# Reordering waits and splits in a two-layer decoder trunk in split float32

## The chip, the cores and the metric

One Trainium2 chip, one core. The metric is the device time of one execution in microseconds (us); lower is better. Times of several executions are given as a median.

## The reference

Two layers run over a sequence of 512 tokens of width 1024. Each layer is one pre-normalised mixer, a residual add, and a gated per-layer embedding:

```python
u = rms_norm(h, norm_g)
z = u @ w_in                       # q,k,v,gate of 8 "fox" heads, forget column, q,k,v,gate of 8 dilated heads
log_f = log_sigmoid(fa + b_f)      # forget logarithm, 8 heads
oa = forgetting_attention(rms_norm(qa), rms_norm(ka), va, log_f) * silu(ga)   # bias: cumulated log_f, causal
ob = dilated_attention(rope(rms_norm(qb)), rope(rms_norm(kb)), vb) * silu(gb)
h = h + concat([oa, ob]) @ w_out
gate = sigmoid(rms_norm(h, ple_norm_g) @ w_ple_gate)
h = h + (p_i @ w_ple) * gate
```

Everything is float32. The kernel keeps that precision on TensorE by cutting each operand into a rounded high half and the low half that is left, and by three products (high by high, high by low, low by high) in place of one.

## The kernel before

**Tiling.** Activations lie transposed, 8 blocks of 128 channels by 512 tokens; the tiles `X` and `Y` each hold a high and a low half of all 8 blocks. The 16 heads are taken as 8 pairs: pairs 0 to 3 are dilated heads, pairs 4 to 7 forgetting heads. Tokens come in 4 tiles of 128.

**Weights.** The class `Weights` (lines 93 to 201) streams them in a fixed order. A piece is loaded by SP into one of 3 `raw` buffers, ScalarE copies it into a high half `whi` (line 159), VectorE subtracts to get the low half `wlo` (line 160). There are 5 slots of halves. `W.pump()` does one piece if a slot is free, and issues the next load; `W.get` does pieces until the one asked for is there. Each piece that is done frees a raw buffer, and so lets the next load go.

**The order of the work.** TensorE's instructions keep the order in which they are written (`InOrder`, line 80). The other engines' instructions are put in order by a planner, which simulates the program at compile time and takes what is ready, what is written earlier first; at run time each engine's queue is then fixed. `with behind("A", "V"):` (line 372) pins what is issued inside it on ScalarE ("A") and VectorE ("V") behind the instructions recorded in `last["A"]` and `last["V"]`. These records are made at a few places only: line 449 (copy of v), 456 and 464 (q and k after the norm and the rotation), 480 (gate), 620 and 621 (halves of the probabilities), 650 and 651 (output of a product with v), 810 (the low half of a weight piece), and 881 (the embedding gate).

**A layer.** First pair 0 is projected (`proj`) into four PSUM banks, two of the pool `psA` and two of `psM`; in layer 0 this goes block by block as the inputs arrive (lines 664 to 692), and for block `d == 0` all four token tiles take one of the three products before the next product begins. Then for p from 1 to 7 (line 753) pair p is projected in four tiles (`pj`, `ev`), the scores and the softmax of pair p - 1 are made (`att_s`), its probabilities are transposed (`att_tp`, `att_tp2`) and split (`att_pt`, `att_pt2`), and pair p - 2 is multiplied with v (`att_pv`) and written out as halves (`att_o`). `bias_causal` adds the causal mask to the bias rows of a forgetting pair in two VectorE instructions (line 529); `att_s` adds the mask rows to the scores and takes the minimum (line 596), ScalarE takes the exponential (598), VectorE a reciprocal (599), GpSimd scales (600).

**The forget logarithm.** `log_forget` (line 484) makes log_f of 128 by 32 elements with two table functions of ScalarE, Exp and Ln; `cumulate`, at p = 4, first splits it (lines 501 and 502) and then sums it along the tokens. `rope_tables(l + 1)` makes the rotation tables of the next layer in 8 VectorE instructions (lines 366 and 367). Both are written into the loop without a pin, at p = 2 and at p = 7.

**The last pair and the output product.** From line 815 on the output product (`part(d, k0, k1)`) runs on the blocks of pairs that are done, between the last steps of attention: `att_pv` of pair 6, `att_o(6)`, the scores of pair 7, `part(0, 6, 7)`, which needs both halves of pair 6's output, `part(2, 0, 5)`, and the transposes of pair 7's probabilities. After the eight output blocks comes the embedding gate, a loop over d: `pgate(d)` is the product with the gate weights into a bank of `psA`, `gated` reads it on VectorE (line 881), ScalarE takes Tanh (882), VectorE multiplies and adds (886, 888); in layer 0 the block is stored (`hs`), split for the next layer (391, 392) and squared. Each d ends with one pump whose instructions on VectorE are pinned behind line 881 of the same d:

```python
                with behind("V"):
                    W.pump()
```

The next layer's first projection starts right after the last `pgate`.

Of the kernel before, what the change touches and what calls it, by code (L numbers as in the profile page):

```python
# [9 lines left out]
F32 = mybir.dt.float32  # L10
F32R = mybir.dt.float32r
I32 = mybir.dt.int32
AF = mybir.ActivationFunctionType
ALU = mybir.AluOpType
# [189 lines left out]
def trunk(tc, ap):  # L204
# [3 lines left out]
    with ctx:  # L208
# [275 lines left out]
        def log_forget(l):  # L484
            t = [sp.tile([P, NT, 8], F32, tag=f"lf{i}", name=f"lf{i}", bufs=1) for i in range(4)]
            y, w, lw, e = t
            V.tensor_scalar(y, fx, -1.0, None, op0=ALU.mult)
            V.tensor_tensor(y, y, fx, op=ALU.max)
            A.activation(y, y, AF.Exp, scale=-1.0)
            V.tensor_scalar(w, y, 1.0, None, op0=ALU.add)  # L490
            A.activation(lw, w, AF.Ln)
            V.tensor_scalar(e, w, 1.0, None, op0=ALU.subtract)
            V.tensor_tensor(e, y, e, op=ALU.subtract)
            V.reciprocal(w, w)
            V.tensor_tensor(e, e, w, op=ALU.mult)
            V.tensor_tensor(lw, lw, e, op=ALU.add)
            V.scalar_tensor_tensor(fx, fx, 0.0, lw, op0=ALU.min, op1=ALU.subtract)

        def cumulate():
            ps = ptile(psM, "psM")  # L500
            A.activation(lf[:, :, 0:8], fx, AF.Copy)
            V.tensor_tensor(lf[:, :, 32:40], fx, lf[:, :, 0:8].bitcast(F32), op=ALU.subtract)
            for t in range(NT):
                n = (NT - t) * P
                T.matmul(ps[0:40, S - n:], lf[:, t], tri[:, :n], start=(t == 0),
                         stop=(t == NT - 1))
            c = tp.tile([8, S], F32, tag="ob", name="c")
            A.activation(c, ps[32:40], AF.Copy)
            V.tensor_tensor(c, ps[0:8], c, op=ALU.add)
            nc.sync.dma_start(cd, c)  # L510
# [15 lines left out]

        def bias_causal():
            for x in (MF[:, 7:20:4], MF[:, 3:13:3]):
                V.tensor_tensor(x, x, causal[:, None, :].to_broadcast([P, NT, P]), op=ALU.add)  # L529

# [119 lines left out]

        def att_o(a, dst):
            V.tensor_tensor(U[7], U[7], U[5 + a % 2], op=ALU.mult)  # L654
            A.activation(dst[0][:, a], U[7], AF.Copy)
            V.tensor_tensor(dst[1][:, a], U[7], dst[0][:, a].bitcast(F32), op=ALU.subtract)  # L656


        gh, oo = X, Y
# [5 lines left out]
        for d in range(NK):  # L665
            if d == 0:
                W.slice_conv()
                with tc.issue_after(W.first.ins):
                    split_gh(gh, U[d], gn[:, 0, d:d + 1], d)
            else:  # L670
                split_gh(gh, U[d], gn[:, 0, d:d + 1], d)
                W.slice_conv()
            if d == 2:
                W.slice_load()
                W.slice_load()
                small_loads()
            tail = square_acc(U[d], d)
            if d == NK - 1:
                while W.load():
                    pass  # L680
                W.pump(PZ)
                stats0 = finish_stats(psS, "psS")
                rope_base(tail)
                rope_tables(0)
            if d == 0:
                wh, wl = (x[:, :QW0] for x in W.cur)
                for i in range(3):
                    for t in range(NT):
                        T.matmul(first[t][:, :QW0], gh[i % 2][:, 0, t * P:(t + 1) * P],
                                 wl if i == 2 else wh, start=i == 0, stop=False)  # L690
            for t in range(NT if d > 0 else 0):
                proj(0, 0, t, gh, first[t], d, d + 1)
        for l in range(DEPTH):
            u = gh
# [57 lines left out]

            for p in range(1, NPAIR):
                a, b = p - 1, p - 2
                if p == 2:
                    log_forget(l)
                if p == 7 and l + 1 < DEPTH:
                    rope_tables(l + 1)
                if p == 1:
                    pj(p, 0)  # L760
                    pj(p, 1)
                    ev(p, 0)
                    att_qk(l, 0, att_z(zt(0)))
                    W.pump(2)
                else:
                    pj(p, 0, 0, 6)
                    att_pv(b, 0)
                    att_pt(1, tps)
                    pj(p, 0, 6, NK)
                    pj(p, 1, 0, 3)  # L770
                    att_pv(b, 1)
                    pj(p, 1, 3, NK)
                    ev(p, 0)
                    with behind("A", "V"):
                        W.pump()
                    att_o(b, oo)
                ev(p, 1)
                if p > 1:
                    with behind("A", "V"):
                        W.pump()  # L780
                if a >= NDIL:
                    with behind("V"):
                        bias_causal()
                pj(p, 2)
                ev(p, 2)
                att_s(a)
                if NDIL <= p < NPAIR and a >= NDIL:
                    bias_rows(p)
                pj(p, 3)
                ev(p, 3)  # L790
                if p == NDIL:
                    cumulate()
                    bias_rows(p)
                gps = ptile(psA, "psA")
                gate_mm(l, p, u, gps, 0, NK)
                with behind("A", "V"):
                    W.pump()
                tps = [pair(psS, "psS") for _ in range(2)]
                att_tp(tps)
                pqk = att_z(zt(p))  # L800
                tpb = ptile(psA, "psA")
                att_tp2(tpb)
                tanh, rest = gate_evac(p, gps)
                att_pt(0, tps)
                with behind("A"):
                    tanh()
                att_pt2(tpb)
                with behind("A", "V"):
                    W.pump()
                last["V"] = W.lo  # L810
                att_qk(l, p, pqk)
                with behind("V"):
                    rest()
# [3 lines left out]
            att_pv(b, 0)  # L817
            att_pt(1, tps)
            with behind("A", "V"):
                W.pump()  # L820
            part(0, 5, 6)
            part(1, 0, 3)
            att_pv(b, 1)
            with behind("A", "V"):
                W.pump()
            part(1, 3, 5)
            att_o(b, oo)
            with behind("V"):
# [39 lines left out]

            def pgate(d, k0, k1, c=slice(0, S)):
                if d not in gps or c.start > 0:  # L870
                    gps[d] = ptile(psA, "psA")
                wh, wl = W.get(("pg", l, d))
                for k in range(k0, k1):
                    mm3(gps[d][:, c], wh[:, k, :], wl[:, k, :], pg[0][:, k, c], pg[1][:, k, c],
# [29 lines left out]
            for d in range(NK):  # L904
# [25 lines left out]
                else:  # L930
# [5 lines left out]
                    for c, th in zip(halves, ths):  # L936
                        ple(d, c)
                        gated_b(d, c, th)
                        nc.sync.dma_start(ap["out"][d][:, c], U[d][:, c])
                with behind("V"):  # L940
                    W.pump()
            gh, oo = nxt, pg


# [54 lines left out]
```

## Time and profile before

| what | value |
|---|---|
| median of 3 runs | 700.66 us (699.09 to 1112.28) |
| the profiled execution, its own time | 699.79 us |
| its span, first to last instruction | 698.0 us |
| mean granted TensorE clock | 0.997 |
| HBM read, written | 70.78 MB, 4.23 MB |
| DMA, mean | 109 GB/s |

A line of the profile that groups instructions gives line, engine, operation, output and inputs by tile name, then busy time and the idle time of the engine ahead of them with what ended it. PE is TensorE's matmuls, PEld its weight loads, DVE VectorE, ACT ScalarE, POOL GpSimd, SPq the queue of SP. `L87` and `L90` are the two helpers through which all matmuls and all transposes go, so these are told apart by their tiles. PE's busy time is modelled, so PE counts as busy between closely spaced matmuls; the start times of its instructions show its real pace.

### The profile page before, as it was taken

What the parts mean: (1) busy time and instruction counts of PE and PEld (TensorE: products, weight loads), DVE (VectorE), ACT (ScalarE), POOL (GpSimd) and SP (SyncE); (2) the same over time, 40 slices, a digit from 0 to 9 for tenths busy, and PEclk for the clock granted to TensorE, in tenths of its full rate; (3) what the DMA queues carried; (4) which work ended last, traced back from release to release, by engine and by line L of the source; (5) the groups of instructions that cost most, each with busy time, mean ns of one, the idle gap of its engine ahead of it and who ended that gap; (6) DMA issues with size and microseconds to landing.
All of it is one profiled execution on the core that took longest, in us unless ns stands there. A gap on an engine that the chain in (4) does not pass through costs nothing.

```text
span 698.0 us, 12101 instructions
## 1 busy us (share of the span) xinstructions
PE 688.7 (99%) x4351; PEld 612.2 (88%) x4351; DVE 512.1 (73%) x1255; ACT 381.2 (55%) x806; POOL 181.0 (26%) x318
## 2 busy tenths in 40 slices
PE   9999999999999999999989999999999999999997
PEld 8998898999989878888789998999989998788887
DVE  7888788777887878638558678777878877784544
ACT  8676556565664766435325566466555756573311
POOL 7462634324131220000003625534041331200000
PEclk9999999999999999999999999999999999999999
DMA  7612232234342444414253032221543533453221
GB/s 254 225 33 69 56 93 66 83 113 156 96 137 98 130 134 154 136 45 146 98 167 121 1 91 65 87 69 54 155 127 111 138 107 120 130 159 105 91 76 46
DMA packets 32172, 75.79 MB, mean 109 GB/s; under 512 B 4832, under 2 KB 12256, under 8 KB 32112
## 3 DMA queue, kind: packets, MB, share of 16 engines
q1 hardware_dynamic: 31824, 75.01, 34.4%
q8 instruction: 34, 0.56, 0.3%
q14 instruction: 26, 0.21, 0.1%
q10 hardware_dynamic: 288, 0.01, 0.0%
HBM read 70.78 MB, written 4.23 MB: 107 GB/s over the span
## 4 chain that ended last, share of the span: by engine, by line
PE 91%; DVE 4%; ACT 2%; issue 1%; POOL 1%; DMA 1%; SPq 0%; DVEq 0%; ACTq 0%; POOLq 0%
PE psA L87 63%; PE psS L87 19%; PE psM L87 4%; PE psS L90 2%; PE psM L90 1%; PE psA L90 1%; DVE wlo L160 1%; ACT U L598 1%; POOL f L443 1%; DMA raw<-in_wq_dram 1%; DVE MF L529 0%; DVE U L596 0%; DVE U L654 0%; ACT whi L159 0%; DVE z L456 0%
## 5 line engine op out<-in xcount | busy, mean ns | idle before, releaser
L159 ACT ACTIVATE whi<-raw 128x1024 fp32r<-128x1024 f32 (+5 forms) x104 | 106.3, 1024 | 63.6 <-PE psA L87 41.9
L160 DVE TENSOR_TENSOR wlo<-raw,whi 128x1024 fp32r<-128x1024 f32 (+3 forms) x105 | 123.3, 1174 | 13.8 <-ACT whi L159 13.0
L87 PE MATMUL psA<-whi,X 128*128 128x384 f32 (+1 forms) x480 | 130.7, 342 | 0.9 <-DVE U L480 0.9
L87 PE MATMUL psA<-whi,Y 128*128 128x384 f32 (+1 forms) x480 | 129.9, 342 | 0.0
L443 POOL TENSOR_TENSOR f<-ms,mhalf 128x4 f32<-128x4 f32 x64 | 64.7, 1011 | 237.7 <-DVE ms L441 228.3
L87 PE MATMUL psA<-Y,whi 128*128 128x512 f32 (+1 forms) x320 | 97.0, 386 | 0.8 <-DVE Y L656 0.7
L87 PE MATMUL psA<-X,whi 128*128 128x512 f32 x304 | 96.3, 397 | 0.8 <-DVE X L656 0.6
L598 ACT ACTIVATE U<-U,mx 128x512 f32<-128x512 f32 (+3 forms) x128 | 70.5, 553 | 40.4 <-DVE mx L596 30.3
L87 PEld LDWEIGHTS psA<-whi,X 128*128 128x128 f32 x480 | 87.4, 188 | 2.2 <-DVE U L480 0.9
L87 PEld LDWEIGHTS psA<-whi,Y 128*128 128x128 f32 x480 | 87.5, 188 | 0.6
L87 PE MATMUL psA<-wlo,X 128*128 128x384 f32 (+1 forms) x240 | 80.9, 338 | 0.2 <-DVE wlo L160 0.2
L87 PE MATMUL psA<-wlo,Y 128*128 128x384 f32 (+1 forms) x240 | 81.0, 338 | 0.0
L600 POOL TENSOR_SCALAR U<-U,sm 128x512 f32<-128x512 f32 (+3 forms) x128 | 65.7, 531 | 51.0 <-DVE sm L599 50.7
L87 PEld LDWEIGHTS psA<-Y,whi 128*128 128x128 f32 x320 | 58.4, 188 | 13.7 <-DVE Y L656 1.0
L87 PEld LDWEIGHTS psA<-X,whi 128*128 128x128 f32 x304 | 56.5, 188 | 14.5 <-DVE X L656 1.0
L87 PE MATMUL psA<-Y,wlo 128*128 128x512 f32 (+1 forms) x160 | 61.1, 382 | 0.0
L87 PE MATMUL psA<-X,wlo 128*128 128x512 f32 x152 | 60.0, 395 | 0.0
L620 ACT ACTIVATE PT<-psS 128x512 fp32r<-128x512 f32 (+1 forms) x58 | 31.3, 590 | 50.9 <-PE psS L90 39.0
L456 DVE TENSOR_TENSOR z<-psA,f 128x256 f32<-128x256 f32 x60 | 25.4, 423 | 40.6 <-POOL f L443 40.6
L405 POOL TENSOR_TENSOR r<-m,mhalf 128x4 f32<-128x4 f32 x4 | 4.7, 1184 | 162.5 <-DVE m L404 162.5
L87 PEld LDWEIGHTS psA<-wlo,X 128*128 128x128 f32 x240 | 45.1, 188 | 0.5 <-DVE wlo L160 0.5
L87 PEld LDWEIGHTS psA<-wlo,Y 128*128 128x128 f32 x240 | 45.2, 188 | 0.0
(187 smaller groups left out, 1240.3 us busy)
## 6 DMA issues: line engine op xcount, KB each, us to landing
raw<-in_wq_dram SPq DMA_DIRECT2D x28, 576.0 KB, 3.9
raw<-in_wg_dram SPq DMA_DIRECT2D x16, 512.0 KB, 3.5
raw<-in_wo_dram SPq DMA_DIRECT2D x16, 512.0 KB, 3.3
raw<-in_wpg_dram SPq DMA_DIRECT2D x16, 512.0 KB, 3.4
raw<-in_wq_dram SPq DMA_DIRECT2D x14, 384.0 KB, 3.2
U<-in_xT_dram SPq DMA_DIRECT2D x16, 256.0 KB, 4.2
MF<-cd SPq DMA_DIRECT2D x16, 256.0 KB, 3.5
MF<-cd SPq DMA_DIRECT2D x16, 192.0 KB, 3.7
```

The lines of the kernel that those rows point to most:

```text
L87: return self.tc.keep_in_program_order(self.eng.matmul(*a, **k))
L90: return self.tc.keep_in_program_order(self.eng.transpose(*a, **k))
L159: self.nc.scalar.activation(hi, r, AF.Copy)
L160: self.lo = eng.tensor_tensor(lo, r, hi.bitcast(F32), op=ALU.subtract)
L405: G.tensor_tensor(r, m, mhalf.to_broadcast([P, NT]), op=ALU.pow)
L443: G.tensor_tensor(f, ms, mhalf.to_broadcast([P, 4]), op=ALU.pow)
L456: last["V"] = V.tensor_tensor(z, ps[:, :2 * P].rearrange("p (h d) -> p h d", h=4), f[:, :, None].to_broadcast([P, 4, HD]), op=ALU.mult)
L598: A.activation(seg, seg, AF.Exp, bias=mx, scale=-1.0, accum_out=sm)
L600: G.tensor_scalar(seg, seg, sm, 1.0, op0=ALU.mult, op1=ALU.mult)
L620: last["A"] = A.activation(hi, src, AF.Copy)
```

## The change

Six edits:

- **The forget logarithm** is called at p = 1, after the first two tiles of pair 1's projection are issued, with its instructions pinned behind the last recorded ones of ScalarE and VectorE (line 449 of pair 0's tile 3, and line 480 of pair 0), and now makes its two split halves itself; `cumulate` no longer does.
- **The rotation tables** of layer 1 are made in layer 0's gate loop at d = 2, pinned behind line 881 of that d, and no longer written at p = 7.
- **The last but one output**: `att_o` and `bias_causal` record their last instructions, so that after the loop the two causal mask adds of pair 7 are pinned behind the low half of pair 6's output.
- **The splits**: the two weight pieces of that stretch are both issued ahead of the second product with v.
- **The gate loop**: `pgate(2)` takes its bank from `psM`; the pump is pinned for d = 0 alone.
- **The first projection**: block 1 too is done product by product over the four token tiles.

```diff
@@ log_forget / cumulate
             V.scalar_tensor_tensor(fx, fx, 0.0, lw, op0=ALU.min, op1=ALU.subtract)
+            A.activation(lf[:, :, 0:8], fx, AF.Copy)
+            V.tensor_tensor(lf[:, :, 32:40], fx, lf[:, :, 0:8].bitcast(F32), op=ALU.subtract)
 
         def cumulate():
             ps = ptile(psM, "psM")
-            A.activation(lf[:, :, 0:8], fx, AF.Copy)
-            V.tensor_tensor(lf[:, :, 32:40], fx, lf[:, :, 0:8].bitcast(F32), op=ALU.subtract)
@@ bias_causal
             for x in (MF[:, 7:20:4], MF[:, 3:13:3]):
-                V.tensor_tensor(x, x, causal[:, None, :].to_broadcast([P, NT, P]), op=ALU.add)
+                last["V"] = V.tensor_tensor(x, x, causal[:, None, :].to_broadcast([P, NT, P]), op=ALU.add)
@@ att_o
             V.tensor_tensor(U[7], U[7], U[5 + a % 2], op=ALU.mult)
-            A.activation(dst[0][:, a], U[7], AF.Copy)
-            V.tensor_tensor(dst[1][:, a], U[7], dst[0][:, a].bitcast(F32), op=ALU.subtract)
+            last["A"] = A.activation(dst[0][:, a], U[7], AF.Copy)
+            last["V"] = V.tensor_tensor(dst[1][:, a], U[7], dst[0][:, a].bitcast(F32),
+                                        op=ALU.subtract)
@@ first projection
-            if d == 0:
-                wh, wl = (x[:, :QW0] for x in W.cur)
+            if d < 2:
+                wh, wl = (x[:, d * QW0:(d + 1) * QW0] for x in W.cur)
                 for i in range(3):
                     for t in range(NT):
-                        T.matmul(first[t][:, :QW0], gh[i % 2][:, 0, t * P:(t + 1) * P],
-                                 wl if i == 2 else wh, start=i == 0, stop=False)
-            for t in range(NT if d > 0 else 0):
+                        T.matmul(first[t][:, :QW0], gh[i % 2][:, d, t * P:(t + 1) * P],
+                                 wl if i == 2 else wh, start=d == 0 and i == 0, stop=False)
+            for t in range(NT if d > 1 else 0):
                 proj(0, 0, t, gh, first[t], d, d + 1)
@@ the loop over pairs
                 a, b = p - 1, p - 2
-                if p == 2:
-                    log_forget(l)
-                if p == 7 and l + 1 < DEPTH:
-                    rope_tables(l + 1)
                 if p == 1:
                     pj(p, 0)
                     pj(p, 1)
+                    with behind("A", "V"):
+                        log_forget(l)
                     ev(p, 0)
@@ after the loop
             att_pv(b, 0)
             att_pt(1, tps)
             with behind("A", "V"):
-                W.pump()
+                W.pump(2)
             part(0, 5, 6)
             part(1, 0, 3)
             att_pv(b, 1)
-            with behind("A", "V"):
-                W.pump()
             part(1, 3, 5)
             att_o(b, oo)
             with behind("V"):
                 bias_causal()
@@ pgate
-                    gps[d] = ptile(psA, "psA")
+                    gps[d] = ptile(psM, "psM") if d == 2 else ptile(psA, "psA")
@@ end of the gate loop
-                with behind("V"):
+                with behind(*("V" if d == 0 else "")):
                     W.pump()
+                if d == 2 and l + 1 < DEPTH:
+                    with behind("V"):
+                        rope_tables(l + 1)
```

## Rows read from the trace of the kernel before

**Rows 1.** The page, busy time, share of the span and instructions of each engine.

```profile
PE 688.7 (99%) x4351; PEld 612.2 (88%) x4351; DVE 512.1 (73%) x1255; ACT 381.2 (55%) x806; POOL 181.0 (26%) x318
```

**Rows 2.** The waits of PE over the span: us in total, times, longest.

```profile
PE psM L87 <- DVE wlo L160: 1.9, 1, 1.9
...
PE psA L87 <- DVE U L480: 0.9, 2, 0.6
...
PE psA L87 <- DVE Y L656: 0.7, 1, 0.7
...
PE psA L87 <- DVE X L656: 0.6, 1, 0.6
```

**Rows 3.** Timeline where layer 0 ends: start, us, engine, line, tiles, count, idle before.

```profile
329.26 1.19 ACT L159 ACTIVATE whi<-raw 128x1176 fp32r<-128x1176 f32 x1
...
348.79 0.69 DVE L881 TENSOR_TENSOR sqh<-psA,Rh 128x512 f32<-128x512 f32 x1 [2.00 <-PE psA L87]
...
349.40 1.38 DVE L160 TENSOR_TENSOR wlo<-raw,whi 128x1176 fp32r<-128x1176 f32 x1
...
350.83 0.45 PE L87 MATMUL psM<-wlo,Y 128*128 128x392 f32 x1 [1.89 <-DVE wlo L160]
```

**Rows 4.** Busy time by stretch; after POOL granted clock, DMA share, GB/s.

```profile
352.00:356.00 4.00, 4.00 (x15) 3.70 (x15) 3.83 (x6) 2.26 (x3) 0.00 (x0) 0.57 0.87 181
```

**Rows 5.** The chain that ended last, one piece: start, us, engine, tile, count.

```profile
268.94 11.15 PE psA L87 x48
```

**Rows 6.** Timeline of the last pair in layer 0, DVE and PE.

```profile
248.61 0.69 DVE L529 TENSOR_TENSOR MF<-MF,cst 128x512 f32<-128x512 f32 x1
...
249.21 0.69 DVE L596 CUSTOM_DVE_ANT_0 U<-psS,MF 128x512 f32<-128x512 f32 x1
...
249.41 0.50 PE L87 MATMUL psA<-Y,whi 128*128 128x512 f32 x1
...
249.82 0.69 DVE L656 TENSOR_TENSOR Y<-U,Y 128x512 fp32r<-128x512 f32 x1
...
250.57 0.50 PE L87 MATMUL psA<-Y,whi 128*128 128x512 f32 x1 [0.65 <-DVE Y L656]
...
255.52 0.71 PE L90 MATMUL psM<-cst,U 64*128 64x64 f32 x16
```

**Rows 7.** Waits from 240 to 262 us, one of them.

```profile
PEld psM L90 <- POOL U L600: 0.5, 1, 0.5
```

**Rows 8.** Timeline of the first pair of layer 0, DVE, PE and ACT.

```profile
40.48 0.88 DVE L561 SCALAR_TENSOR_TENSOR KK<-psM,gq,KK 128x256 fp32r<-128x256 f32 x2
...
43.02 1.50 PE L87 MATMUL psS<-KK,QQ 64*128 64x512 f32 x12
...
43.85 1.28 ACT L491 ACT_TABLE_LOAD   x1
...
46.69 0.72 ACT L598 ACTIVATE U<-U,mx 128x512 f32<-128x512 f32 x1
...
58.01 0.45 PE L87 MATMUL psA<-whi,X 128*128 128x384 f32 x1 [0.62 <-DVE U L480]
```

**Rows 9.** Busy time on tile lf, the forget logarithm, in layer 0 and 1.

```profile
41.00:54.00 13.00, 0.00 (x0) 0.00 (x0) 2.96 (x10) 0.69 (x3) 0.00 (x0) 1.00 0.08 29
...
381.00:386.00 5.00, 0.00 (x0) 0.00 (x0) 1.96 (x10) 0.69 (x3) 0.00 (x0) 1.00 0.33 105
```

**Rows 10.** Timeline of pair 3 in layer 0, DVE and PE.

```profile
115.73 0.49 DVE L366 TENSOR_TENSOR Cg<-cosT,gr 128x64 f32<-128x64 f32 x3
...
117.38 0.41 PE L87 MATMUL psA<-whi,X 128*128 128x384 f32 x1 [0.28 <-DVE U L480]
```

**Rows 11.** Timeline of PE where the third gate product of layer 0 begins.

```profile
308.95 0.40 PE L87 MATMUL psS<-QQ,wlo 128*128 128x512 f32 x1
...
309.37 0.72 PE L87 MATMUL psA<-X,whi 128*128 128x512 f32 x2
```

**Rows 12.** Timeline of PE in the first projection, second k step.

```profile
7.38 0.45 PE L87 MATMUL psA<-wlo,X 128*128 128x392 f32 x1 [0.16 <-DVE wlo L160]
```

## The prediction

> **What bounds the kernel now.** I read the busy times first: TensorE is busy for 99% of the span, the next engine for 73% [rows 1]. So a change that keeps all 4351 matmuls can save only time in which TensorE waits or is slow. The second view is the list of TensorE's waits: 4.1 us in five waits behind VectorE [rows 2]; the longest, 1.9 us, is where layer 0 hands over to layer 1. The third view is the granted clock by stretches: a mean of 0.997 over the span, but 0.57 from 352 to 356 us, right behind that longest wait [rows 4]. A mean of 0.57 is TensorE mostly at 1.2 GHz in place of 2.4: it does 57% of the work that it could, so (1 - 0.57) x 4 us = 1.7 us are lost. Waits and slow clock together are 5.8 us, 0.8% of the run. That is nearly all there is to win, and each part of the change can be set against one of these places.
>
> **The layer boundary.** The next layer's first weight piece had its high half at 329.26 us, but its low half began only at 349.40, right behind the gate instruction of line 881 at 348.79, though VectorE had been idle for 2.00 us ahead of that one [rows 3]. That is the pin: the piece belongs to the pump of d = 7 (until then no slot counts as free), so its low half sits behind line 881 of d = 7, which waits for the last gate product. TensorE wants it at once and waits 1.89 us [rows 3]; then comes the clock at 0.57. Without the pin the planner can put this subtraction, 1.38 us long, into any VectorE gap of the 20 us between. I take the wait and the slow stretch as both gone: 1.9 + 1.7 = 3.6 us. Bounds: 0, if the planner still writes it late; 3.6. I take the upper end, since the pump's ScalarE half, which carries no pin, ran 19 us ahead. Earlier subtractions also free raw buffers, so SP issues loads earlier, among the stores of h; layer 1 reads those stores only at its own end, so nothing waits. What is late next is the last block's square for the new statistics, wanted only after 84 products of the projection; I cost it 0.
>
> **The last but one output, twice.** TensorE starts a product with pair 6's high half at 249.41 and the next, which needs the low half, at 250.57, although a product of 512 columns takes 11.15 / 48 = 0.23 us [rows 5, 6]: 0.93 us lost. The low half is made at 249.82, after the second causal add (248.61) and the first mask add (249.21) [rows 6]. Afterwards the adds stand behind the low half, and the second weight split, which also sat in front, is done while attention's product still runs. So this wait goes. But does the time come back? A few products on, TensorE comes to the transposes of pair 7's probabilities, at 255.52, and the profile shows a weight load of theirs waiting for GpSimd's scaling [rows 6, 7]: the softmax is already the later of the two. TensorE, 0.93 us early, will wait there for it. The softmax itself starts when the mask adds do. The first add moves back behind low half and both causal adds, but the second no longer has the low half between it and the first; since the exponentials follow one another on ScalarE, the second add's start decides. Counting instructions ahead of the second add leaves it about 0.15 us earlier. Bounds: +0.6 (one instruction of 0.69 us more ahead, less overlap) to -0.93. I take -0.15, twice (layer 1 repeats the pattern, its wait is the 0.6 in [rows 2]): 0.3 us. What waits behind the newly pinned adds: the mask adds and reciprocals on VectorE, then ScalarE's exponentials and GpSimd's scaling.
>
> **The forget logarithm.** In layer 0 the planner had pulled it up to pair 1 anyway: it stands between the scores and the softmax, with two table loads of 1.28 us on ScalarE between 43.85 and the first exponential at 46.69 [rows 8], and 2.96 us of VectorE work from 41 us on [rows 9]. All behind it runs late, so line 480 frees its bank late and TensorE waits 0.62 us at 58.01 [rows 8]. Moved up behind line 480 of pair 0, only one table load is left ahead of the softmax: gain 0.62. The price is at the scores: KK's low half ends at 41.36 and TensorE starts the scores at 43.02, a slack of 1.66 us [rows 8]; 10 VectorE and 3 ScalarE instructions now go in front. Layer 1 shows this already: there they stood at 381 us ahead of the scores, took 1.96 us of VectorE [rows 9], and no wait of TensorE is listed. By that row the excess is 1.96 - 1.66 = 0.3 us; by layer 0's 2.96 it is 1.3; with ScalarE's 0.69 and one load of 1.28 in one chain with it, 3.3. The least is 0, if gaps take them. I take 0.3, the row of the same position. Net gain 0.3. In layer 1 I take no change, with the same upper bound.
>
> The Trainium skill, page "ScalarE: Activation LUTs", section "What ACT_TABLE_LOAD costs", gives a switch 1.28 us for the load and about 1.38 more for a drain. That would speak against this edit: by it the switch in front of the scores costs 1.38 us more and the sum is 696.1. The trace does not agree: two loads and the Ln between them fit into 2.84 us [rows 8].
>
> **The rotation tables.** They too had been pulled up, to pair 3: eight small VectorE instructions, three of them at 115.73 taking 0.49 us, ahead of line 480, and TensorE waits 0.28 us for that at 117.38 [rows 10]. Gone with the move: 0.3. At the new place they take some 1.3 us (eight at that rate) of VectorE ahead of the rest of d = 2; TensorE's next claim on this work is a bank two gate products later, 48 x 0.23 = 11 us, so 0. If that cover were gone it would cost the 1.3.
>
> **The small ones.** pgate(2): 308.95 to 309.37 is 0.42 [rows 11], 0.19 more than a product; two layers, 0.4 us, bounds 0 and 0.4. The psM banks were read long before. First projection: a wait of 0.16 us at 7.38 for the low half [rows 12], which now has four products more of time: 0.2, bounds 0 and 0.3. The records in att_o and bias_causal inside the loop are overwritten by `ev` before any pin reads them: 0. No matmul, no DMA is added.
>
> **The sum.** Against the profiled execution's own 699.79 us (span 698.0; the median of the runs shown is 0.9 higher): 3.6 + 0.3 + 0.3 + 0.3 + 0.4 + 0.2 = 5.1, so 694.7.
>
> **Rivals.**
> - *The clock falls at the moved wait.* In both tails TensorE now waits about 0.8 us in one piece ahead of the transposes, which are short work. Behind 1.89 us the clock fell, behind 0.65 it didn't [rows 2, 4]; this lies between, nearer the harmless one. Two falls at 1.7 us: 698.1.
> - *The boundary wait stays or is replaced*, because the planner writes the low half late all the same or another half is late in its place: 3.6 us back, 698.3. Against it: idle VectorE ahead of 348.79 [rows 3].
> - *The tails keep their gain*, since the softmax moves up with the output: 2 x (0.93 - 0.15) = 1.6 more, 693.1. The wait for GpSimd [rows 7] speaks against the full amount.
> - *Slower: the logarithm blocks the first scores.* Its chain alternates between ScalarE and VectorE, and both run in order, so QQ and KK queue behind a copy that waits for the whole chain. At the upper bound of 3.3 us a layer, and the clock falling behind so long a wait (1.7), two layers cost 10.0 in place of 0.3: 704.4. It turns the sign once a layer loses over 2.7 us. Against it: layer 1's position, without a wait.
> - *Nothing changes*: the pins were not what held the order, 699.8. The 19 us between the two halves speak against it.
>
> **How the numbers follow.** Forecast 0.56; clock in the tails 0.12; boundary 0.10; tails kept 0.14; blocked scores 0.05; nothing 0.03. The time is the forecast's, 694.7. The range 691.9 to 699.0 takes in the first four and the bounds of the terms (below, the tails' full gain, the logarithm free and a run 0.7 us under its profile, as the lowest of before was); it leaves out the last two and some mixtures, 2 in 10 at most. Two per cent, 14 us, is about what a measurement of this kernel tells from no change: no case wins that (5.8 us of waits and slow clock in all), and none here loses it; I leave 0.02 on either side for what I have not seen, and 0.96 within.
>
> **What would show it.** Right: no wait for `wlo` at the handover and a granted clock of 1.0 through it; no wait for line 656, and a wait of about 0.8 us for GpSimd ahead of the transposes in both layers; no wait for line 480 in pairs 1 and 3; TensorE's scores of pair 0 starting within half a us of the previous products' end. Wrong: a stretch at 0.57 anywhere else, a gap ahead of the first scores, or a low half still behind line 881 of d = 7.

## The result and the profile after

| | before | after |
|---|---|---|
| median, run side by side | 699.19 us (6 executions) | 694.82 us (6 executions) |
| profiled execution, its own time | 699.79 us | 694.84 us |
| its span | 698.0 us | 693.1 us |
| mean granted clock | 0.997 | 1.000 |

The ratio is 0.9933, 95% interval 0.992 to 0.9947: 0.7% faster, inside the 2% that count as no change. One of the six executions before took 1112.28 us; it stands in the median and not in the ratio. The forecast was 694.7 us.

The waits of TensorE after the change (us in total, times, longest), against [rows 2]:

```profile
PE psM L90 <- POOL U L600: 2.3, 2, 1.2
PE psM L87 <- DVE ones L305: 1.0, 1, 1.0
PE psA L87 <- DVE z L456: 0.5, 1, 0.5
PE psA L87 <- ACT whi L159: 0.3, 1, 0.3
```

All waits for line 656, line 480 and `wlo` are gone. Three are new: GpSimd's scaling ahead of the transposes in both layers, `z` in layer 0, and a high half in the first projection. The one for `ones` stands at the start in both kernels.

The handover of layer 0 to layer 1, busy time by stretch (after the engines the granted clock, DMA share, GB/s), against 0.57 in [rows 4]:

```profile
348.00:352.00 4.00, 4.00 (x24) 3.99 (x23) 3.34 (x4) 1.77 (x3) 0.00 (x0) 1.00 0.17 37
352.00:356.00 4.00, 4.00 (x24) 4.00 (x23) 1.35 (x2) 1.04 (x2) 0.00 (x0) 1.00 0.43 170
```

And its timeline (start, us, engine, line, tiles, count, idle before), against [rows 3]:

```profile
328.19 1.38 DVE L160 TENSOR_TENSOR wlo<-raw,whi 128x1176 fp32r<-128x1176 f32 x1 [1.50 <-ACT whi L159]
...
336.06 1.38 DVE L160 TENSOR_TENSOR wlo<-raw,whi 128x1176 fp32r<-128x1176 f32 x1
...
347.91 0.34 PE L87 MATMUL psM<-whi,Y 128*128 128x392 f32 x1
348.09 0.35 PE L87 MATMUL psM<-wlo,Y 128*128 128x392 f32 x1
```

The subtraction runs at 328 us, 20 us before it is wanted, and that of the second weight piece at 336 us. TensorE passes from the first product to the one with `wlo` in 0.18 us, where it waited 1.89.

**Where the time went.** Both kernels issue the same 4351 matmuls, so the start of each can be set against the start of the same one before; a step is the place where this difference changes. The last column sets the trace after against a second trace of the kernel before, which the last experiment gave.

| place | forecast | first trace before to after | second trace before to after |
|---|---|---|---|
| start, first projection | -0.2 | +0.59 | +0.53 |
| pair 1 and the gate behind it, layer 0 | -0.3 | +0.62 - 0.80 = -0.18 | +0.58 - 0.84 = -0.26 |
| pair 3, layer 0 | -0.3 | -0.53 | -0.53 |
| last pair, layer 0 and layer 1 | -0.15, -0.15 | -0.21, -0.20 | -0.22, -0.22 |
| third gate product, two layers | -0.4 | -0.56 | -0.57 |
| handover | -3.6 | -3.76 | -2.39 |
| sum of these | -5.1 | -4.85 | -3.66 |
| end of the last matmul | | -4.92 | -3.95 |

### The profile page after: what moved, and what is told of

It is laid out like the page before. It is cut to its first block, busy times and chain, and to the rows that moved or that the text cites. A ratio compares the mean times of both kernels' runs of the same rounds, so it can differ in the third digit from the quotient of the medians.

```text
span 693.1 us, 12100 instructions
## 1 busy us (share of the span) xinstructions
PE 685.1 (99%) x4351; PEld 611.2 (88%) x4351; DVE 511.1 (74%) x1255; ACT 380.1 (55%) x806; POOL 181.0 (26%) x318
## 4 chain that ended last, share of the span: by engine, by line
PE 93%; DVE 2%; ACT 1%; POOL 1%; DMA 1%; issue 1%; SPq 0%; DVEq 0%; POOLq 0%
PE psA L87 64%; PE psS L87 18%; PE psM L87 6%; PE psS L90 3%; PE psM L90 1%; PE psA L90 1%; POOL U L600 1%; DMA U<-in_xT_dram 1%; DMA raw<-in_wo_dram 0%; DVE U L596 0%; DVE wlo L160 0%; ACT whi L159 0%; DVE MF L529 0%; DVE U L651 0%; ACT X L391 0%
## 5 line engine op out<-in xcount | busy, mean ns | idle before, releaser
L87 PE MATMUL psA<-Y,whi 128*128 128x512 f32 (+1 forms) x304 | 91.5, 384 | 0.0
L87 PE MATMUL psA<-X,whi 128*128 128x512 f32 x288 | 90.8, 396 | 0.0
L87 PEld LDWEIGHTS psA<-Y,whi 128*128 128x128 f32 x304 | 55.5, 188 | 11.3
L87 PEld LDWEIGHTS psA<-X,whi 128*128 128x128 f32 x288 | 53.5, 188 | 11.9
L87 PE MATMUL psA<-Y,wlo 128*128 128x512 f32 (+1 forms) x152 | 58.0, 381 | 0.0
L87 PE MATMUL psA<-X,wlo 128*128 128x512 f32 x144 | 56.7, 394 | 0.0
```

The source lines that it names most:

```text
L87: return self.tc.keep_in_program_order(self.eng.matmul(*a, **k))
```

## The experiments

The theory after the result: the handover's pin was worth the 1.9 us wait and the slow clock behind it; the tails' gain moves to the transposes, because the softmax of pair 7 is late; the logarithm's price fell on a bank; the tables' and the bank's gains are real; the start differs from execution to execution. Each of these was tried by itself, but for the bank of the third gate product, which is read from the traces alone. Where executions are counted by their clock, it is the mean granted clock over the span that each timed execution reports.

**1. The pin of the pump alone, on the kernel before.**

```diff
-                with behind("V"):
+                with behind(*("V" if d == 0 else "")):
                     W.pump()
```

> The kernel before with one edit: the pump of the gate loop is pinned for d = 0 alone. My theory (the pin alone made the boundary wait, and the slow clock followed from the wait): no wait for wlo at the handover, a granted clock of 1.0 there, 3.6 to 3.8 us less than the kernel before (ratio 0.9947); the waits of pairs 1 and 3 and of the last but one output stay as they were. Rival (it takes the move of the rotation tables or the psM bank too, since they take VectorE time and TensorE order in the same loop): under 2 us less. Rival (the clock fell for another reason than the wait): 1.9 us less, with 0.57 still seen near 350 us.

Measured: 696.93 us (695.97 to 697.17) against 699.15 beside it, ratio 0.9964 (0.9952 to 0.9976): 2.2 us, less than expected. PE at the handover and the stretch behind it:

```profile
349.49 0.35 PE L87 MATMUL psM<-wlo,Y 128*128 128x392 f32 x1
```

```profile
350.00:354.00 4.00, 4.00 (x25) 3.99 (x23) 2.89 (x5) 1.77 (x4) 0.00 (x0) 1.00 0.28 99
```

The wait and the slow stretch are both gone, and within the traces the handover is 3.76 us shorter, as expected. That the medians differ by 2.2 only is taken up in experiment 10.

**2. The pin put back, in the changed kernel.**

```diff
-                with behind(*("V" if d == 0 else "")):
+                with behind("V"):
                     W.pump()
```

> The changed kernel with that one edit undone: the pump of every d is pinned behind line 881's place again. My theory: the wait of about 1.9 us for wlo and the clock at half for some 3.4 us come back, 3.6 to 3.8 us more than the changed kernel, so about 1.1 us under the kernel before. Rival (other edits of the change freed the boundary): within 1 us of the changed kernel.

Measured: 698.31 us (696.65 to 699.18), ratio to before 0.9981 (0.997 to 0.9991), 3.5 us over the changed kernel. Its waits and its stretch behind the handover:

```profile
PE psM L87 <- DVE wlo L160: 1.9, 1, 1.9
```

```profile
352.00:356.00 4.00, 4.00 (x16) 3.82 (x15) 3.89 (x6) 2.19 (x3) 0.00 (x0) 0.62 0.87 254
```

Wait and slow clock return together: this one edit carries most of the change. Its 11 executions fall into 8 with a clock of 0.996 or 0.997 (698.7 in the mean) and 3 at 0.999 (697.1).

**3. The tails alone, on the kernel before**: the records in `att_o`, behind which the causal adds are then pinned, and the two splits ahead of the second product. The record in `bias_causal` is not part of it.

```diff
-            A.activation(dst[0][:, a], U[7], AF.Copy)
-            V.tensor_tensor(dst[1][:, a], U[7], dst[0][:, a].bitcast(F32), op=ALU.subtract)
+            last["A"] = A.activation(dst[0][:, a], U[7], AF.Copy)
+            last["V"] = V.tensor_tensor(dst[1][:, a], U[7], dst[0][:, a].bitcast(F32),
+                                        op=ALU.subtract)
...
-                W.pump()
+                W.pump(2)
...
-            with behind("A", "V"):
-                W.pump()
```

> The kernel before with the tail's edits alone: att_o and bias_causal's pin behind the low half, and both weight splits ahead of the second product with v. My theory (the softmax of the last pair is the later of the two, so the wait only moves): no wait for line 656, a wait of 1.0 to 1.3 us for GpSimd ahead of the transposes in each layer, 0.2 to 0.5 us less than the kernel before in all. Rival (the time comes back): 1.9 us less or more. Rival (the clock falls behind the moved wait): 1.7 us more per fall.

Measured: 699.89 us (698.01 to 700.65) against 699.15, ratio 1.0005 (0.9993 to 1.0016). The medians can't tell, since either kernel has executions of both clocks. Among executions at 0.999 or 1.0 it is 698.44 (5) against 698.93 (16), among those at 0.998 or less 700.30 (7) against 700.65 (7): 0.35 to 0.5 us less, and the last matmul of its trace, which has the slow stretch behind the handover as that of before, starts 0.39 earlier. Its waits show the move:

```profile
PE psM L90 <- POOL U L600: 2.3, 2, 1.2
```

Both waits for line 656 are gone, and the transposes wait 1.1 us in each layer instead. TensorE is 1.3 us earlier behind the output product, and of this 0.19 us is left behind the transposes, in each layer.

**4. The causal adds of pair 7 straight after the loop, without a pin.**

```diff
             a, b = NPAIR - 1, NPAIR - 2
+            bias_causal()
             part(0, 0, 5)
...
             att_o(b, oo)
-            with behind("V"):
-                bias_causal()
             att_s(a)
```

> The changed kernel with one edit: the two causal adds of the last pair are written right after the loop, ahead of the output product, without a pin. If the softmax chain is what TensorE waits for at the transposes, its first mask add starts 1 to 2 us earlier and the wait of 1.1 us goes in both layers: 2.0 to 2.6 us less than the changed kernel (about 692.4). If the wait hangs on GpSimd's or ScalarE's own pace from the scores on, under 0.5 us. If the adds push pair 6's halves or the attention output on VectorE, the wait for the low half comes back, up to 1 us per layer, and the time is the changed kernel's or more.

Measured: 704.17 us (702.77 to 704.67), ratio to before 1.0065 (1.0052 to 1.0079): some 9 us slower than the changed kernel, the opposite of what was expected. Timeline of VectorE and TensorE in layer 0, and the stretch behind:

```profile
233.38 0.69 DVE L529 TENSOR_TENSOR MF<-MF,cst 128x512 f32<-128x512 f32 x1 [2.75 <-DMA MF<-cd]
...
236.55 0.42 DVE L456 TENSOR_TENSOR z<-psA,f 128x256 f32<-128x256 f32 x1 [0.91 <-POOL f L443]
...
237.03 0.34 PE L90 MATMUL psM<-cst,z 64*128 64x64 f32 x4 [1.98 <-DVE z L456]
...
238.85 1.19 PE L87 MATMUL psA<-Y,whi 128*128 128x512 f32 x2 [0.90 <-DVE U L480]
```

```profile
240.00:244.00 4.00, 4.00 (x11) 3.13 (x10) 3.75 (x7) 2.26 (x5) 0.00 (x0) 0.50 0.20 74
```

The planner pulled the add forward to where the mask rows were still on their way: VectorE stands still for 2.75 us for that transfer, and with it all that is queued behind, up to `z` of pair 7. TensorE waits 1.98 and 0.90 us, then runs at 1.2 GHz. In layer 1 the same happens with a wait of 3.88 us for the transfer. The theory of the softmax was not tested by this; the placing was wrong.

**5. The same adds in VectorE's gaps.** One add behind the split of the probabilities (long after the transfer), one behind the product with the gate, while ScalarE makes the high half; the mask adds pinned behind the low half. The new arguments of `bias_causal` and `att_o` are not shown.

```diff
...
             att_pt(1, tps)
+            with behind("V"):
+                bias_causal(0, 1)
...
-            att_o(b, oo)
-            with behind("V"):
-                bias_causal()
-            att_s(a)
+            att_o(b, oo, lambda: bias_causal(1, 2))   # between the product and its halves
+            with behind("V"):
+                att_s(a)
```

> The changed kernel, with the two causal adds of pair 7 in VectorE's gaps, one behind the split of the first probabilities (line 621), one behind the product with the gate (line 654), and the mask adds pinned behind the low half. Theory (the softmax of pair 7 is what the transposes wait for, and its start is set by the adds that stand behind the low half): the first mask add starts at about 248.1 us in place of 249.25, the wait of 1.1 us for GpSimd ahead of the transposes falls to 0.2 us or less in both layers, and the time is 1.8 to 2.2 us less than the changed kernel's, about 692.8. Rival 1 (the exponentials or GpSimd's own queue set the end): the wait stays at 1.1, no difference. Rival 2 (VectorE is full there): the low half comes late instead, a wait of 0.5 us or more for line 659, and half of the gain is lost.

Measured: 693.05 us (692.72 to 693.35), ratio to before 0.9909 (0.9896 to 0.9923). Timeline of its VectorE and PE (line 659 is 656):

```profile
241.73 0.68 DVE L529 TENSOR_TENSOR MF<-MF,cst 128x512 f32<-128x512 f32 x1
...
246.80 0.68 DVE L529 TENSOR_TENSOR MF<-MF,cst 128x512 f32<-128x512 f32 x1
247.58 0.69 DVE L659 TENSOR_TENSOR Y<-U,Y 128x512 fp32r<-128x512 f32 x1
248.19 0.68 DVE L596 CUSTOM_DVE_ANT_0 U<-psS,MF 128x512 f32<-128x512 f32 x1
...
254.03 0.71 PE L90 MATMUL psM<-cst,U 64*128 64x64 f32 x16 [0.17 <-POOL U L600]
```

The first mask add starts at 248.19 in place of 249.25, and the transposes wait 0.17 us in place of 1.11. TensorE gains 0.94 and 0.85 us at the two transposes, and behind the start it gains or loses no more than 0.1 us anywhere else. So the softmax of pair 7 was the later one, and the two adds in front of it set its start. This version beats both kernels (the changed one side by side in experiment 9).

**6. The forget logarithm one tile later**, written after `ev(p, 0)`.

```diff
-                    with behind("A", "V"):
-                        log_forget(l)
                     ev(p, 0)
+                    with behind("A", "V"):
+                        log_forget(l)
```

> The changed kernel, with the forget logarithm written after the evacuation of pair 1's first token tile in place of ahead of it. Theory (two of its instructions push line 441 of that tile behind the gate's multiply, so z is late and the bank of that tile is freed late): the wait of 0.55 us for z at about 39.8 us goes, TensorE is 0.6 us earlier from there on in layer 0, and the time is 0.5 to 0.6 us less than the changed kernel's. Rival (the logarithm's work is in the way wherever it stands): a wait of 0.5 us or more at the scores of pair 0 or at the bank of the next tile takes its place, no difference.

Measured: 694.09 us (693.83 to 694.8), ratio to before 0.9925 (0.9913 to 0.9938), not told apart from the changed kernel's 0.9933. Against the trace of the changed kernel TensorE is 0.62 us earlier at the bank of pair 1 and loses 0.53 again at the scores of pair 0. ScalarE and TensorE there:

```profile
41.04 1.28 ACT L491 ACT_TABLE_LOAD   x1
42.33 0.23 ACT L491 ACTIVATE lf<-lf 128x32 f32<-128x32 f32 x1
42.47 0.46 ACT L560 ACTIVATE KK<-psM,gq 128x256 fp32r<-128x256 f32 x1
```

```profile
44.39 1.26 PE L87 MATMUL psS<-KK,QQ 64*128 64x512 f32 x10 [0.25 <-DVE KK L561]
```

The second half of KK stands behind the table load, so the scores wait for it: the rival.

**7. The rotation tables back at p = 7, without a pin.**

```diff
+                if p == 7 and l + 1 < DEPTH:
+                    rope_tables(l + 1)
...
-                if d == 2 and l + 1 < DEPTH:
-                    with behind("V"):
-                        rope_tables(l + 1)
```

> The changed kernel, with the rotation tables written at p = 7 again and without a pin. Theory (the planner pulls the eight instructions up to pair 3, ahead of line 480): they stand there again, TensorE waits 0.3 us for line 480 at about 117 us, and the time is 0.3 to 0.5 us more than the changed kernel's. Rival (the wait in pair 3 came from the late logarithm): no wait, no difference.

Measured: 694.51 us (694.32 to 695.23), ratio to before 0.9932 (0.9919 to 0.9944). The tables stand in pair 3 again, in front of line 480:

```profile
115.11 0.49 DVE L366 TENSOR_TENSOR Cg<-cosT,gr 128x64 f32<-128x64 f32 x3
...
115.93 0.68 DVE L480 TENSOR_TENSOR U<-psA,Rh 128x512 f32<-128x512 f32 x1
```

TensorE loses 0.24 us at that place against the changed kernel, less than expected, and no wait of its for line 480 is listed; the time can't show it. So the tables are worth about half of the 0.53 us found at pair 3. In the trace before, VectorE also stood idle for 0.20 us ahead of the weight split in front of them; what brought that was not tried.

**8. Block 1 of the first projection tile by tile again.**

```diff
-            if d < 2:
+            if d < 1:
...
-            for t in range(NT if d > 1 else 0):
+            for t in range(NT if d > 0 else 0):
```

> The changed kernel, with block 1 of the first projection done token tile by token tile again. Theory (the start is set by when block 1 of the input lands, which differs by 1 us from run to run, and the low half is 0.16 us late in the old order): the time is 0 to 0.2 us more than the changed kernel's, less than these rounds can tell. Rival (the new order itself costs the 0.6 us that TensorE was late there in the profile of the changed kernel): 0.6 us less.

Measured: 694.68 us (694.47 to 694.96), ratio to before 0.9933 (0.992 to 0.9945): no difference from the changed kernel. The old wait is back, and its time is not:

```profile
7.95 0.45 PE L87 MATMUL psA<-wlo,X 128*128 128x392 f32 x1 [0.24 <-DVE wlo L160]
```

At the 121st matmul the traces with the new order start 0.59, 0.21, 0.45, 0.48, 0.62, 0.71, -0.12, 0.21 and -0.14 us after the first trace of before (mean 0.33), those with the old order 0.00, 0.73, 0.03, 0.10 and 0.57 (mean 0.29). Two things go with a late start. In five traces, 0.45 to 0.73 us late, ScalarE waited 0.46 to 1.19 us for block 1 to land, as in the trace after:

```profile
6.22 0.72 ACT L391 ACTIVATE X<-U,gn 128x512 fp32r<-128x512 f32 x1 [1.12 <-DMA U<-in_xT_dram]
```

In those of experiments 2 and 5, 0.71 and 0.48 us late, it did not wait. There TensorE's first products follow each other at 0.32 us for longer, until 6.97 and 6.35 us, and at 0.18 us afterwards; 0.33 us is also the pace of such products in the slow stretch behind the handover. The first line is of experiment 2, the second of the first trace of before:

```profile
5.70 0.85 PE L87 MATMUL psM<-whi,X 128*128 128x392 f32 x2
```

```profile
5.10 0.52 PE L87 MATMUL psM<-whi,X 128*128 128x392 f32 x2
```

That the clock rose later there is inferred from this pace and not shown: the clock column of the profile has 1.00 for the stretch. Of the seven traces that are left, the four with the new order are 0.04 us late in the mean and the three with the old order 0.04 too.

**9. The logarithm at p = 2 in place of p = 1, on top of 5**, pinned behind the last exponential and reciprocal of pair 1's softmax (the two records for this, in `att_s`, are not shown); run beside 5 once more and the changed kernel once more.

```diff
-                    with behind("A", "V"):
-                        log_forget(l)
...
                 ev(p, 3)
+                if p == 2:
+                    with behind("E", "R"):   # last exponential and reciprocal
+                        log_forget(l)
```

> The kernel with the causal adds in VectorE's gaps, and the forget logarithm moved once more: to p = 2, pinned behind the last exponential of pair 1's softmax, where ScalarE is idle for 3.2 us (83.15 to 86.38 in the trace of that kernel). Theory (the logarithm costs TensorE time only where its table loads and VectorE steps stand ahead of a bank or of the scores): the wait of 0.5 us for z at 40 us goes and none takes its place at the scores of pair 0 or behind 86 us, and the time is 0.5 to 0.9 us less than that kernel's, about 692.3. Rival (two table loads are late somewhere wherever they stand): the splits of pair 1's probabilities (line 620, 86.4 us) or the gate of pair 2 come late, a wait of 0.5 us or more there, no difference.

> The kernel with the causal adds in VectorE's gaps, once more, to be compared on the same chip: 693.0 within 0.5 us, by every theory.

> The changed kernel once more, to be compared on the same chip: 694.8 within 0.5 us by every theory, and 1.8 us over the kernel with the causal adds in the gaps. If the start is set by when the second input block lands, its profile shows the first products of that block 0 to 1 us apart from the earlier profile's and no other difference over 0.2 us.

Measured: 695.94 us (695.61 to 696.53) with the logarithm at p = 2, 692.65 (692.32 to 692.9) for version 5 and 694.7 (693.9 to 695.05) for the changed kernel; ratios to before 0.9953 (0.9939 to 0.9966), 0.9905 (0.989 to 0.992) and 0.9933 (0.9919 to 0.9946). The move is a miss, 3.3 us slower than version 5; the two repeats came as expected, and the second trace of the changed kernel differs from the first by 0.39 us at the start and by no more than 0.1 behind it. Timeline of ScalarE, VectorE and PE of the first of them:

```profile
82.82 0.23 ACT L491 ACTIVATE lf<-lf 128x32 f32<-128x32 f32 x1
...
83.08 0.35 DVE L494 RECIPROCAL lf<-lf 128x32 f32<-128x32 f32 x1 [0.92 <-ACT lf L491]
...
86.63 0.34 PE L90 MATMUL psM<-cst,z 64*128 64x64 f32 x4 [0.36 <-DVE z L464]
...
88.59 0.42 PE L87 MATMUL psA<-whi,X 128*128 128x384 f32 x1 [1.04 <-DVE U L480]
```

The first wait, for `z` at 40 us, did go: 0.6 us against one trace of version 5, 0.8 against the other. But VectorE stands for 0.92 us until ScalarE's Ln is done, with the last tile of pair 2 queued behind it; `z` and the gate come late, and TensorE loses 1.7 to 1.8 us in each layer. ScalarE was idle there; VectorE's queue was not.

**10. The kernel before once more.**

> The kernel before, once more. Of its 43 executions timed so far beside other kernels, 12 show a mean granted clock of 0.998 or less and take 700.5 us in the mean, 31 show 0.999 or 1.0 and take 699.0. Theory (the clock falls behind the wait of 1.89 us at the handover in some executions only): if this profile's clock is 0.999 or 1.0, it shows the same wait for the low half at about 350 us and no stretch under 0.9 behind it, and a time near 699; if it is 0.998 or less, the stretch from 352 to 356 us is near 0.57 again and the time near 700.5. Rival (the wait itself is shorter in the faster executions): a wait of 0.5 us or less there at a time near 699.

Measured: 699.26 us (698.68 to 700.69), ratio 1.000 (0.9991 to 1.001). The profiled execution took 698.82 us at a clock of 1.0. PE at the handover and the stretch behind:

```profile
350.95 0.45 PE L87 MATMUL psM<-wlo,Y 128*128 128x392 f32 x1 [1.89 <-DVE wlo L160]
```

```profile
352.00:356.00 4.00, 3.98 (x22) 3.66 (x21) 3.88 (x6) 2.20 (x3) 0.00 (x0) 1.00 0.84 216
```

The same wait of 1.89 us, and no slow stretch. So the clock falls behind this wait in some executions only. Over the 66 executions of this kernel in the runs of experiments 1 to 10, 18 have a mean clock of 0.998 or less and take 700.46 us in the mean, 48 have 0.999 or 1.0 and take 698.99. Where the clock fell is seen in traces only: the three with this wait and a mean of 0.997 (before, experiments 2 and 3) have the slow stretch right behind the handover and no other listed before the last matmul.

Without the slow stretch the pin still costs more than the wait in the list, because the low half of the second weight piece is late with it: the load of that piece into TensorE waits once more (PEld in this trace).

```profile
352.85 0.19 PEld L87 LDWEIGHTS psM<-wlo,Y 128*128 128x128 f32 x1 [0.34 <-DVE wlo L160]
```

Against this trace the handover of the changed kernel is 2.39 us shorter. That explains experiment 1: its five executions take 696.77 us in the mean, 2.2 less than the 698.93 of those of before beside them that are at 0.999 or 1.0, and the slow stretch, some 1.5 us, is saved only in the executions that have it.

Of the 89 executions of the three kernels with this wait, 33 have a mean clock of 0.998 or less (18 of 66, 8 of 11 in experiment 2, 7 of 12 in experiment 3); of the 46 of kernels without it, experiment 4 left out, none has. Why the share differs among the three was not tried.

## Why the prediction was right, and where it was not

**The bound.** Right: all that was won came out of TensorE's waits and the slow stretch, and none of the other engines' work mattered but where it stood in front of a bank or an operand.

**The handover.** The mechanism was right, and the size right for the profiled execution: 3.76 us against 3.6. As a price in every execution it was too large. The step that failed is "I take the wait and the slow stretch as both gone: 1.9 + 1.7 = 3.6": the slow stretch was, by the mean clock, in 18 of 66 executions, and the 1.9 leaves out the second low half, so that what is there always is 2.39 us, by the second trace. The forecast time was not hurt, because it was subtracted from a profiled execution that had the slow stretch, and none of the 12 timed executions of the changed kernel has a mean clock under 0.999.

**The tails.** Right in sign, place and nearly in size: 0.2 us a layer for 0.15. The wait ahead of the transposes was 1.11 and 1.15 us, not the 0.8 forecast. The 0.93 us that the prediction takes for TensorE's loss at the output is only the gap ahead of the low half; the product before it was late too, by 0.29 us (248.89 to 249.41 where a product takes 0.23), since the high half was ready at 249.36 only (248.73 + 0.63). PE and ScalarE before the change:

```profile
248.89 0.40 PE L87 MATMUL psA<-Y,wlo 128*128 128x512 f32 x1
```

```profile
248.73 0.63 ACT L655 ACTIVATE Y<-U 128x512 fp32r<-128x512 f32 x1 [2.27 <-DVE U L654]
```

So TensorE came 1.3 us earlier to the transposes; less the 0.2 that was kept, this is the 1.1 measured. VectorE and PE of layer 0 after the change:

```profile
247.44 0.69 DVE L656 TENSOR_TENSOR Y<-U,Y 128x512 fp32r<-128x512 f32 x1 [0.70 <-ACT Y L655]
248.05 1.29 DVE L529 TENSOR_TENSOR MF<-MF,cst 128x512 f32<-128x512 f32 x2
249.25 0.68 DVE L596 CUSTOM_DVE_ANT_0 U<-psS,MF 128x512 f32<-128x512 f32 x1
...
255.10 0.72 PE L90 MATMUL psM<-cst,U 64*128 64x64 f32 x16 [1.11 <-POOL U L600]
```

The low half is now first, but the mask adds start at 249.25, where the first one started at 249.21 in [rows 6]. Experiment 5 shows that this start was the price. The rival of a falling clock at the moved wait did not come: no stretch there is slow behind 1.1 us.

**The forget logarithm.** The net is near (0.2 to 0.3), the path was wrong. The gain at line 480 came (0.8 us). The step that failed is "The price is at the scores": it fell one step earlier, at the bank of pair 1's third tile, 0.6 us. Before the change, VectorE:

```profile
35.69 0.23 DVE L441 TENSOR_SCALAR ms<-ms,E 128x4 f32<-128x4 f32 x1
...
36.53 0.69 DVE L481 SCALAR_TENSOR_TENSOR U<-sqh,U 128x512 f32<-128x512 f32 x1 [0.48 <-ACT sqh L481]
```

After the change, VectorE, GpSimd, PE and ScalarE:

```profile
36.00 0.17 DVE L487 TENSOR_SCALAR lf<-fx 128x32 f32<-128x32 f32 x1
...
36.62 0.18 DVE L488 TENSOR_TENSOR lf<-lf,fx 128x32 f32<-128x32 f32 x1
...
37.12 0.69 DVE L481 SCALAR_TENSOR_TENSOR U<-sqh,U 128x512 f32<-128x512 f32 x1 [0.32 <-ACT sqh L481]
...
37.87 0.22 DVE L441 TENSOR_SCALAR ms<-ms,E 128x4 f32<-128x4 f32 x1
...
38.24 1.01 POOL L443 TENSOR_TENSOR f<-ms,mhalf 128x4 f32<-128x4 f32 x1 [3.67 <-DVE z L464]
...
39.28 0.43 DVE L456 TENSOR_TENSOR z<-psA,f 128x256 f32<-128x256 f32 x1 [0.80 <-POOL f L443]
...
39.85 0.41 PE L87 MATMUL psA<-whi,X 128*128 128x384 f32 x1 [0.55 <-DVE z L456]
...
39.34 0.84 ACT L553 ACTIVATE QQ<-psM,gq 128x256 fp32r<-128x256 f32 x2
40.20 1.28 ACT L491 ACT_TABLE_LOAD   x1
41.50 0.23 ACT L491 ACTIVATE lf<-lf 128x32 f32<-128x32 f32 x1
```

Two instructions of the logarithm, together 0.35 us, pushed line 441 behind line 481, which itself waits for ScalarE; before, line 441 ran ahead of line 481. GpSimd's factor and `z` follow it, and `z` frees the bank. In experiment 6 line 441 is ahead of line 481 again (36.77 and 37.15), and this wait is gone. Experiments 6 and 9 show that the price moves with the logarithm and was not got rid of: to the scores, or to the next pair.

The Trainium skill, page "ScalarE: Activation LUTs", section "What ACT_TABLE_LOAD costs", puts a drain of about 1.38 us on top of the load at every switch. The traces show none on either side of a load: here it starts 0.02 us after the end of the activation ahead of it (39.34 + 0.84 = 40.18), and the Ln 0.02 us after the load's end (40.20 + 1.28 = 41.48); in the trace before, each of the six loads has 0.02 us ahead of it and 0.01 us behind it.

Of the rivals none came: the wait at the handover went, the tails kept only the part forecast, and the scores start right behind the product ahead of them, with no wait of theirs in the list above.

**The rotation tables and the bank of the third gate product.** Right in sign and place. For the tables 0.24 us is shown by experiment 7, where 0.3 was forecast; the rest of the 0.53 found at pair 3 has another cause, which stays open. For the bank it is 0.56 in place of 0.4. That this is the bank's is argued: experiments 1, 3 and 7, which leave the bank alone, move that place by 0.02 us at most. At d = 2 the tables cost TensorE nothing.

**The first projection.** Wrong: 0.2 us forecast, nothing found. The step that failed is "which now has four products more of time: 0.2": the wait for the low half is real, but removing it gives no time, and the start scatters by 0.9 us from execution to execution, whichever order it has.

**The sum.** It came out nearer than its terms. From the first trace before to the trace after the last matmul moved by 4.92 us, against 5.1 forecast; the start was 0.8 us worse than forecast and pair 1 0.1, while pair 3, the tails, the bank and the handover were 0.1 to 0.2 better each. That these made up for the start is luck.

## What to carry to other kernels

A wait that is removed pays only up to the next operand that is late; look for that operand first, and move what stands in front of it, into a gap in which its own inputs have long landed. An instruction put into an in-order queue costs what the instruction behind it is worth, not its own length: 0.35 us cost 0.6 here, and one add in each layer that waited for a transfer cost 9 in all, with the slow clock behind it. A slow stretch in one profile should be weighed by the share of executions that have it.

## What was not expected of the hardware

- By their mean granted clock, it fell behind the same wait of 1.89 us in 18 of 66 executions and not in the other 48; behind 1.1 us it fell in no trace here, and behind 1.98 and 0.90 us close together it was 0.50 from 240 to 244 us.
- The start of the kernel scatters by up to 0.9 us between executions. In five traces the second input block landed late (in the trace after, ScalarE waited 1.12 us for it, in that of before not at all); in two others TensorE's first products kept the slower pace of 0.32 us each for longer.
